# Order of the recurrence's square roots, of the first up-projection operands and of the right operands in a hybrid decoder layer

## The chip, the cores and the metric

The kernel runs on one core of a Trainium2 chip. The metric is the device time of one execution in microseconds (us). Before the change, three runs gave 1567.91, 1569.7 and 1569.8 us, median 1569.7.

A core has five engines that run side by side, each with its own queue, taken in order: TensorE (PE: matmuls, and PEld, its weight loads), VectorE (DVE), ScalarE (ACT), GpSimd (POOL, used here only to issue DMAs that add while they copy) and SyncE (SP, which issues the other DMAs). An instruction waits at the head of its queue until the semaphores it names have been raised; what stands behind it waits too.

## The reference

One layer on x of 1024 positions by 1024 channels, all in float32:

```
h = rms_norm(x, g_mix);  z = h @ w_in + b_in        # 7168 columns: va, ga, xb, gb, sa, sb
u = silu(layer_norm(conv31(va * sigmoid(ga))));  y_a = u @ w_a_out
v = conv4(xb)                                        # 1536 channels
r, i = sigmoid(v @ w_rg_a + b), sigmoid(v @ w_rg_x + b)   # block diagonal, 16 heads of 96
log_a = -8 r softplus(-lam);  a = exp(log_a);  mult = sqrt(-expm1(2 log_a)), 1 at the first position
h_t = a_t h_(t-1) + mult_t i_t v_t                   # the recurrence
y_b = (h * gelu(gb)) @ w_b_out
x1 = x + (sigmoid(sa) * y_a + sigmoid(sb) * y_b) @ w_o
x2 = x1 + relu(rms_norm(x1, g_mlp) @ w_1)^2 @ w_2
out = rms_norm(x2, g_final)
```

## The kernel before

Every float32 operand of a matmul is kept as a high and a low part in the matmul's own format, and a product is three matmuls (high x high, high x low, low x high). The high part is a conversion on ACT; the low part is a subtraction on DVE, or, in `split_dma` (L63 to L67), a negated copy on ACT (L65) to which a DMA issued by POOL adds the source (L66), followed by the high part on ACT (L67). Larger products are done by a Strassen-like scheme: seven block products, numbered p = 1 to 7, whose left and right operands are sums of blocks.

The order on each engine is written out by hand (`manual_schedule`): the instructions stand in the queues in the order in which the program names them. Only the place of the convolution's taps among other work on DVE is set by a plan: `clk` holds estimated times of PE, ACT and DVE, `later` (L640) puts work with a due time on a list, and `vector_work` (L644) and `fill` (L385) put as many taps ahead of each piece of work as its due time leaves room for. A tap is one multiply-add over some 500 elements (L581). A convolution is begun by two scaled copies on ACT (L563, L564).

**Stage one** (L746 to L803) goes through slots s = 3 to 27. In a slot PE does one chunk of z, 128 channels by 1024 positions, as 48 matmuls of 128x512 (`chunk_mm`, L661): 32 with the high part of the chunk's weights, `win_h`, then 16 with the low part, `win_l`. Slots with a head add twice six matmuls of 96x512 for its two gates (`head_mm`, L472); the gates' PSUM tile `rg` exists once, so the second gate's matmuls wait until ACT has read the first (`head_gate`, L482 to L486). In the slot ACT also takes the chunk before out of PSUM (`xb_out`, L415 to L422: bias, then the first tap of the width-4 convolution; its three other taps are on DVE, L430), makes the weights of the next slot (`w_parts`, L656), and the parts of v (`xb_parts`, L436), which wait for the taps on DVE.

The heads come in four groups of four, and after each group stand two slots for the recurrence of its three tiles of 128 channels: in the first (EXP in L740) `scan_exp` (L497) does three times an Exp and a Tanh at the end of ACT's work in that slot; in the second `scan_root` (L506) does three square roots (L510), last in ACT's work of that slot. Exp and Tanh, Sqrt, and the sigmoid each need their own function table, which ACT loads when the kind changes. `scan_tile` (L517) on DVE then does the scan of a tile; its due time in the plan comes from `rooted`, which `scan_root` sets. In the fourth group the slot after Exp and Tanh has no xb chunk to take out and no head behind it.

**The MLP's first steps.** `gseq` (L1110) runs the products of w_a_out, of w_o and the first two block products of w_1 ("u", p = 1 and 2, for the first four pairs of column blocks); GX (L1483 to L1512) lists by step what else is put into the queues. At the steps u0 and after, x1 of the odd positions is transposed to rows (`x1_rows`, L1284: PE, squares on ACT, copies on DVE), its root is found (`x1_root`, L1310; `x1_diag`, L1318), a PE step spreads it over all partitions (`x1_spread`, L1331, tile `rbm`), and eight products on DVE normalize x1 (`x1_normed`, L1341). Then come the sums of the right operand (`g_t`, L1132; n = 1 to 4), their parts (`g_parts`, L1121: operands gu6, gu5, gu7, gu3 by ACT and DVE, gu4 by `split_dma`) and the left operands of the first two pairs (`up_load`, L1373, loads a block of w_1; `up_lhs`, L1383, makes the sums s1, s2, s4 on DVE and the parts by `split_dma`). The tiles for these sums are five in all. `useq` (L1580) then runs the other block products: for the first two pairs p = 6, 5, 7, 3, 4 in turn (PSUM tiles f0b, f1b, f0c, f1c, f0d, f1d, and f0c, f1c, f0d, f1d again), then the pairs 2, 3 and so on (f2b is the first); UX (L1583) lists what goes beside its first steps. PE begins f0b right behind the last "u" product.

Of the kernel before, what the change touches and what calls it, by code (L numbers as in the profile page):

```python
# [30 lines left out]
def trunk_kernel(ctx: ExitStack, tc: tile.TileContext, x, xt_in, xt_eo, vecs, w_in, w_a_out, w_b_out,  # L31
# [15 lines left out]
    def PS(name, tag="ps"):  # L47
        return pp.tile([P, S], F32, tag=tag, name=name, bufs=1 if tag == "ps2" else 3)
# [330 lines left out]
    def at(e, cost, ready=0.0):  # L379
        clk[e] = max(clk[e], ready) + cost  # L380
        return clk[e] + 0.1
# [33 lines left out]
    def xb_out(t, ps):  # L415

        a = T(f"xb{t}")
        nc.scalar.activation(a, ps, AF.Identity, bias=bin_c[:, XB + t:XB + t + 1])
        v = T(f"v{t}")
        w = WB - 1  # L420
        nc.scalar.activation(v, a, AF.Identity, scale=cbw_c[:, w * 12 + t:w * 12 + t + 1],  # L421
                             bias=cbb_c[:, t:t + 1])  # L422
        ready = at("A", 2.35)
        vt[t] = v

        def rest():
            for d in range(1, WB):

                w = WB - 1 - d
                nc.vector.scalar_tensor_tensor(v[:, d:S], a[:, 0:S - d],  # L430
                                               cbw_c[:, w * 12 + t:w * 12 + t + 1], v[:, d:S],
                                               ALU.mult, ALU.add)

        later(ready, 3.8, rest)
# [37 lines left out]
    def head_mm(n, gi):  # L472
        vh, vl = parts[n]
        gh, gl = gws[n]
        gps[n, gi] = ps = PS(f"rg{n}_{gi}", "ps2")
        for hf, hs in enumerate(HALVES):
            o = ps[:HD, hs]
            nc.tensor.matmul(o, gh[:, gi, :], vh[:, hs], start=True, stop=False)
            nc.tensor.matmul(o, gl[:, gi, :], vh[:, hs], start=False, stop=False)
            nc.tensor.matmul(o, gh[:, gi, :], vl[:, hs], start=False, stop=True)  # L480
        at("P", 6 * MM)

    def head_gate(n, gi, ready):
        g, hh = divmod(n, 4)
        a = H(f"g{n}_{gi}", "g")
        nc.scalar.activation(a, gps.pop((n, gi))[:HD, :], AF.Sigmoid,  # L486
                             bias=(ba_c, bx_c)[gi][:, n:n + 1])
        at("A", 1.11, ready)
        for (ti, p0, p1, d0) in PIECES[hh]:
            t = 3 * g + ti  # L490
            if (gi, t) not in gate:
                gate[gi, t] = T(f"g{gi}_{t}")
            nc.sync.dma_start(gate[gi, t][p0:p1, :], a[d0:d0 + p1 - p0, :])
# [12 lines left out]
    def scan_root(g):  # L506
        at("A", 2.56)
        for t in range(3 * g, 3 * g + 3):
            r = gate[0, t]
            nc.scalar.activation(r, r, AF.Sqrt)  # L510
            rooted[t] = at("A", 1.06)
# [17 lines left out]
    def u_out(j, psv, psg):  # L529

        u = T(f"u{j}")
        uv = u.rearrange("p (o n) -> p o n", o=2)
        nc.scalar.activation(uv, psg.rearrange("p (n o) -> p o n", o=2), AF.Sigmoid,
                             bias=bin_c[:, GA + j:GA + j + 1])
        later(at("A", 1.11), 1.28, nc.vector.scalar_tensor_tensor, uv,
              psv.rearrange("p (n o) -> p o n", o=2), bin_c[:, VA + j:VA + j + 1], uv,
              ALU.add, ALU.mult)
        ut[j] = u
        fresh.append(j)
# [104 lines left out]
    def vector_work(end):  # L644
        for ready, _, cost, f, a in sorted(todo, key=lambda x: x[:2]):
            dve(cost, ready, f, *a)
        todo.clear()
        taps["wait"] += fresh
        fresh.clear()
        fill(end)  # L650

    def w_load(s):
        if s < NC1:
            wraw[s] = load_w(w_in[CH[s]], f"win{s}")

    def w_parts(s):  # L656
        if s < NC1:
            wst[s] = split_w(wraw.pop(s), [P, 8, P], f"win{s}")
            at("A", 2.1)

    def chunk_mm(s, n0, n1):  # L661

        wh, wl = wst[s]
        if n0 == 0:
            zps[s] = PS(f"z{s}")
        pairs = [x for k in range(8) for x in ((wh, k, 0), (wh, k, 1))] + [(wl, k, 0) for k in range(8)]
        for n in range(n0, n1):
            w, k, part = pairs[n]
            for hf in range(2):
                nc.tensor.matmul(zps[s][:, HALVES[hf]], w[:, k, :], xw[k][part][hf],  # L670
                                 start=n == 0, stop=n == 23)
        at("P", 2 * (n1 - n0) * MM)
# [67 lines left out]
    EXP = {head_slot: g for g, head_slot in enumerate(HS0[4 * g + 3] + 1 for g in range(4))}  # L740
# [5 lines left out]
    with tc.manual_schedule(engines=ENGINES):  # L746
        for s in range(3, NC1):
            w_load(s + 2)
            taps["hold"] = s > NC1 - 4
            begun = clk["P"]  # L750
            clk["A"], clk["V"] = max(clk["A"], begun + 0.5), max(clk["V"], begun - 2)

            chunk_mm(s, 0, 18)
            before, new, nxt = (head_at.get(s + d) for d in (-1, 0, 1))
            if before is not None:

                head_gate(before, 0, begun)
                head_mm(before, 1)
            chunk_mm(s, 18, 24)
            if new is not None:  # L760
                head_mm(new, 0)

            c = CH[s - 1]
            if s == 3:
                xb_out(0, zps[0])
            if c >= XB:
                xb_out(c - XB, zps[s - 1])
            elif c >= GA:
                u_out(c - GA, zps[s - 2], zps[s - 1])
            w_parts(s + 1)  # L770
            if s == 3 or c >= XB:
                vector_work(0)
                xb_parts(0 if s == 3 else c - XB)
            if before is not None:
                head_gate(before, 1, clk["P"] - 12 * MM)
            if nxt is not None:
                head_w_parts(nxt)
            if s + 2 in head_at:
                head_w(head_at[s + 2])
            for d in range(5):  # L780
                if s - d in EXP:
                    g = EXP[s - d]
                    if d == 0:
                        scan_exp(g)
                        scan_in(begun + 3.5, 3 * g, 3 * g + 1)
                    elif d == 1:
                        scan_in(begun + 3.5, 3 * g + 2)
                        scan_root(g)

                    t = 3 * g + d - (2 if g < 3 else 1)  # L790
                    if 3 * g <= t < 3 * g + 3 and t < 11:
                        later(rooted[t], 4.8, scan_tile, t)
            if s == NC1 - 1:
                z_get(0, z_lhs)
                z_get(1, z_lhs)
            for f, *a in XS.get(s, ()):
                f(*a)
            if s == NC1 - 3:
                for i in range(4):
                    z_load(i // 2, i % 2)  # L800
            vector_work(clk["P"] - 0.7)
            if nxt is not None:
                head_load(nxt)  # L803
# [676 lines left out]
    def g_get(n, f):  # L1480
# [18 lines left out]
        10: ((g_t, "o", 0, 4), (x_in2, 1, 2, 3)), 11: ((g_t, "o", 1, 4),), 12: ((g_parts, "o", 4, 0),),  # L1499
        13: ((g_parts, "o", 4, 1),), 15: ((g_parts, "o", 5, 0),), 16: ((g_parts, "o", 5, 1), (up_load, 0, (0,))),  # L1500
        17: ((g_parts, "o", 3, 0), (up_load, 1, (0,))), 18: ((g_parts, "o", 3, 1), (up_load, 2, (0,))),
        19: ((up_load, 3, (0,)),), 20: ((x1_rows, 0, 1),), 21: ((x1_rows, 2, 3),), 22: ((x1_diag, 0),),
        23: ((x1_spread, 0), (x1_normed, 0, 0)), 24: ((g_parts, "u", 1, 0), (g_parts, "u", 1, 1)),
        25: ((x1_normed, 1, 0),), 26: ((g_parts, "u", 2, 0),), 27: ((g_parts, "u", 2, 1),)}.items()})
    u0 = 2 * o0
    GX.update({u0 + n: v for n, v in {
        0: ((x1_rows, 4, 5, 6, 7),), 1: ((up_load, 0, (1,)),),
        2: ((x1_diag, 1), (x1_spread, 1), (up_load, 1, (1,))),
        3: ((x1_normed, 0, 1), (x1_normed, 1, 1), (g_t, "u", 0, 1), (g_t, "u", 1, 1)),
        4: ((g_t, "u", 0, 2), (g_t, "u", 1, 2)), 5: ((g_parts, "u", 6, 0), (up_lhs, 0, 6)),  # L1510
        6: ((g_parts, "u", 6, 1), (up_lhs, 1, 6), (g_parts, "u", 5, 0), (up_lhs, 0, 5)),
        7: ((g_parts, "u", 5, 1), (up_lhs, 1, 5), (g_t, "u", 0, 3), (g_t, "u", 1, 3))}.items()})  # L1512
    with tc.manual_schedule(engines=ENGINES):
        for j in range(8):
            clk["A"], clk["V"] = max(clk["A"], clk["P"] + 0.5), max(clk["V"], clk["P"] - 2)
# [48 lines left out]
        for n in range(len(gseq) + 1):  # L1564
# [15 lines left out]
    useq = [(i, p) for p in ORDER[1:4] + (3, 4) for i in range(2)]  # L1580
    useq += [(i, p) for i in range(2, AHEAD) for p in ORDER[1:4] + (3, 4)]
    useq += [(i, p) for i in range(AHEAD, NP) for p in ORDER]
    UX = {0: ((g_parts, "u", 7, 0), (g_t, "u", 0, 4)), 1: ((g_parts, "u", 7, 1), (g_t, "u", 1, 4)),  # L1583
          2: ((g_parts, "u", 4, 0),), 3: ((g_parts, "u", 3, 0), (g_parts, "u", 4, 1)),
          4: ((g_parts, "u", 3, 1),)}
    KC = 2
    NC_ = NP // KC
    BLK = {11: 0, 22: 1, 21: 2, 12: 3}
# [88 lines left out]
    with tc.manual_schedule(engines={mybir.EngineType.Activation, mybir.EngineType.DVE,  # L1677
                                     mybir.EngineType.PE}):
        for n in range(len(useq)):
# [4 lines left out]
            while ready < min(len(useq), n + look + 1):  # L1684
# [4 lines left out]
                ready += 1  # L1689
            for f, *a in UX.get(n, ()):  # L1690
                f(*a)
# [111 lines left out]
    g = g_  # L1803
# [141 lines left out]
```

## Time and profile before

| | |
|---|---|
| median of three runs | 1569.7 us (1567.91 to 1569.8) |
| the profiled execution | 1569.0 us, span of its instructions 1567.0 us |
| granted TensorE clock, mean | 0.997 |
| PE busy | 1543.2 us, 98% of the span |
| ACT, DVE, POOL busy | 893.5, 1211.7, 187.5 us |
| DMA | 309.38 MB, mean 197 GB/s |
| longest waits of PE | 7.1 us at the start (for the first squares on ACT), then 2.0 us in three pieces at `rg` |

A line of a timeline gives the start in us from the span's start, the length in us, the engine, the line of the kernel, the operation, output<-inputs by the program's names without buffer numbers, partitions x elements, how many; in brackets the idle time of that engine just before, and what ended it. Matmuls follow each other before the one before has left the array, so a matmul that is listed with 0.39 us takes 0.227 us of PE's time in a row of its like. A line of the waits gives who waited for what, and then us in total, times, and the longest.

### The profile page before, as it was taken

To read this page: it belongs to the slowest core of one execution; us is meant where nothing else is said; L and a number is where in the kernel's file an instruction comes from. 1 tells how busy PE (TensorE), PEld (TensorE's weight loads), DVE (VectorE), ACT (ScalarE), POOL (GpSimd) and SP (SyncE) were. 2 spreads that over 40 slices of the span, in tenths; PEclk is the share of its full clock that TensorE was granted. 3 is DMA by queue.
4 is the path that set the end of the run, shared out by engine and by line. 5 is a ranking of instruction groups with operands and counts; after the bars stand their busy time and mean duration, and the time that the engine had idled before them with its cause. 6 is when DMAs were issued, how large, how long until landed. Compare 5 with 4: busy or idle time off the path is not lost. (4 is left out here: it accounts for less than half of the span.)

```text
span 1567.0 us, 19218 instructions
## 1 busy us (share of the span) xinstructions
PE 1543.2 (98%) x6830; PEld 1267.1 (81%) x6830; DVE 1211.7 (77%) x1631; ACT 893.5 (57%) x1251; POOL 187.5 (12%) x222
## 2 busy tenths in 40 slices
PE   8999999999999999999999999999999999999997
PEld 6888778788888888888888887788888888888886
DVE  6799999979999997468579868765555558888897
ACT  5547575667667666445275777544444475555552
POOL 0000000002222222000022323000000001111110
PEclk9999999999999999999999999999999999999999
DMA  9667878899998878953579878533333779888852
GB/s 371 166 156 185 227 177 219 206 279 233 240 248 214 192 188 233 315 177 108 179 203 304 195 170 201 172 108 108 108 108 114 239 224 228 219 225 227 203 122 107
DMA packets 128799, 309.38 MB, mean 197 GB/s; under 512 B 12944, under 2 KB 30864, under 8 KB 128704
## 3 DMA queue, kind: packets, MB, share of 16 engines
q1 hardware_dynamic: 97824, 230.59, 44.9%
q0 software_dynamic: 30736, 77.31, 27.1%
q8 instruction: 53, 0.87, 0.2%
q14 instruction: 42, 0.34, 0.1%
q10 hardware_dynamic: 144, 0.26, 0.1%
HBM read 147.69 MB, written 58.72 MB: 132 GB/s over the span
## 5 line engine op out<-in xcount | busy, mean ns | idle before, releaser
L670 PE MATMUL z<-xh,win_h 128*128 128x512 f32 x400 | 123.4, 390 | 0.0
L670 PE MATMUL z<-xl,win_h 128*128 128x512 f32 x400 | 123.2, 389 | 0.0
L1738 DVE TENSOR_TENSOR acc<-acc,d 128x1024 f32<-128x1024 f32 x72 | 87.8, 1220 | 33.3 <-PE d L1726 32.7
L670 PE MATMUL z<-xh,win_l 128*128 128x512 f32 x400 | 98.1, 391 | 0.0
L670 PEld LDWEIGHTS z<-xh,win_l 128*128 128x128 f32 x400 | 75.0, 188 | 17.2 <-DMA win_l<-win_raw 0.4
L581 DVE SCALAR_TENSOR_TENSOR y<-u,vec,y 128x511 f32<-128x511 f32 (+14 forms) x120 | 88.5, 737 | 0.0
L670 PEld LDWEIGHTS z<-xh,win_h 128*128 128x128 f32 x400 | 75.1, 188 | 16.2
L670 PEld LDWEIGHTS z<-xl,win_h 128*128 128x128 f32 x400 | 75.1, 188 | 15.8
L486 ACT ACTIVATE g<-rg,vec 96x1024 f32<-96x1024 f32 x32 | 35.6, 1111 | 84.5 <-PE rg L480 46.6
L581 DVE SCALAR_TENSOR_TENSOR yt<-u,vec,yt 128x511 f32<-128x511 f32 (+6 forms) x112 | 82.7, 738 | 0.0
L581 DVE SCALAR_TENSOR_TENSOR y<-yt,csum,y 128x511 f32<-128x511 f32 (+6 forms) x112 | 82.7, 738 | 0.0
L66 POOL DMA_DIRECT2D win_l<-win_raw x25 | 21.8, 872 | 315.4 <-ACT win_l L65 239.0
L1410 ACT ACTIVATE o<-s 128x512 fp32r<-128x512 f32 x56 | 33.8, 624 | 44.8 <-DVE s L1395 29.7
L430 DVE SCALAR_TENSOR_TENSOR v<-xb,vec,v 128x1023 f32<-128x1023 f32 (+2 forms) x36 | 46.2, 1282 | 16.5 <-ACT v L421 15.7
L1024 PE MATMUL yb<-hgh,wb_h 128*128 128x512 f32 x168 | 52.6, 394 | 0.0
L66 POOL DMA_DIRECT2D zo<-zw x42 | 36.8, 878 | 127.3 <-ACT zo L65 114.8
L1024 PE MATMUL yb<-hgl,wb_h 128*128 128x512 f32 x168 | 51.8, 389 | 0.0
L66 POOL DMA_DIRECT2D db_1l<-wr x7 | 6.1, 876 | 309.8 <-ACT db_1l L65 253.9
L1024 PE MATMUL yb<-hgh,wb_l 128*128 128x512 f32 x168 | 41.0, 389 | 0.0
L65 ACT ACTIVATE zo<-zw 128x512 fp32r<-128x512 f32 x42 | 26.3, 625 | 20.7 <-PE z5f L841 2.1
L1024 PEld LDWEIGHTS yb<-hgh,wb_h 128*128 128x128 f32 x168 | 31.5, 188 | 7.4 <-issue 1.0
L990 DVE TENSOR_TENSOR o<-s,o 128x512 fp32r<-128x512 f32 x56 | 37.3, 683 | 0.0
(1778 smaller groups left out, 4666.2 us busy)
## 6 DMA issues: line engine op xcount, KB each, us to landing
w_raw<-in_w_dram SPq DMA_DIRECT2D x34, 512.0 KB, 5.6
fr<-fd SPq DMA_DIRECT2D x32, 512.0 KB, 5.8
wr<-in_w_dram SPq DMA_DIRECT2D x32, 512.0 KB, 6.6
zw<-in_w_in_dram SPq DMA_DIRECT2D x28, 512.0 KB, 5.8
win_raw<-in_w_in_dram SPq DMA_DIRECT2D x25, 512.0 KB, 7.1
win_l<-win_raw POOLq DMA_DIRECT2D x25, 512.0 KB, 6.1
zo<-zw POOLq DMA_DIRECT2D x42, 256.0 KB, 5.7
gates<-zg SPq DMA_DIRECT2D x32, 256.0 KB, 3.9
```

Source lines behind the costliest of these rows:

```text
L65: nc.scalar.activation(l, src, AF.Copy, scale=-1.0)
L66: nc.gpsimd.dma_start(l, src, accum_op=ALU.add)
L430: nc.vector.scalar_tensor_tensor(v[:, d:S], a[:, 0:S - d], cbw_c[:, w * 12 + t:w * 12 + t + 1], v[:, d:S], ALU.mult, ALU.add)
L486: nc.scalar.activation(a, gps.pop((n, gi))[:HD, :], AF.Sigmoid, bias=(ba_c, bx_c)[gi][:, n:n + 1])
L581: nc.vector.scalar_tensor_tensor(o[:, k:], a[:, 0:HS - k], c, o[:, k:], ALU.mult, add)
L670: nc.tensor.matmul(zps[s][:, HALVES[hf]], w[:, k, :], xw[k][part][hf], start=n == 0, stop=n == 23)
L990: tt(l, src, h.bitcast(F32), ALU.subtract)
L1024: nc.tensor.matmul(ps[hf], a, b[:, HALVES[hf]], start=n == 0, stop=n == len(todo) - 1)
L1410: nc.scalar.activation(o[:, 0], src, AF.Copy)
L1738: tt(acc[p, q2], acc[p, q2], ps, ALU.add)
```

## The change

Three moves; no instruction is added or taken away. First, `scan_root` is called ahead of the slot's other ACT work instead of behind it: it stands between the slot's first matmuls and `xb_out`, so that the roots follow the last Tanh directly on ACT. Its estimate `rooted` is earlier with it, and so more taps stand ahead of some work on DVE; in the fourth group the two copies that begin a convolution then stand ahead of the roots on ACT. Second, w_1's odd blocks of the first two pairs are loaded eight steps earlier, and the left operands p = 6 and 5 of these pairs are made one to five steps after u0 instead of five to seven, the first two of them (p = 6) beside the root of x1. Third, in UX the seventh operand's two parts are made at once, then the third's, and the fourth sum (`g_t` 4) and the fourth operand behind them.

```
@@ stage one @@
                 head_mm(before, 1)
+            if s - 1 in EXP:
+                scan_root(EXP[s - 1])
             chunk_mm(s, 18, 24)
...
                     elif d == 1:
                         scan_in(begun + 3.5, 3 * g + 2)
-                        scan_root(g)
@@ GX, from o0 = 28 @@
-        19: ((up_load, 3, (0,)),), 20: ((x1_rows, 0, 1),), 21: ((x1_rows, 2, 3),), 22: ((x1_diag, 0),),
+        19: ((up_load, 3, (0,)),), 20: ((x1_rows, 0, 1),), 21: ((x1_rows, 2, 3), (up_load, 0, (1,))), 22: ((x1_diag, 0), (up_load, 1, (1,))),
@@ GX, from u0 = 56 @@
-        0: ((x1_rows, 4, 5, 6, 7),), 1: ((up_load, 0, (1,)),),
-        2: ((x1_diag, 1), (x1_spread, 1), (up_load, 1, (1,))),
+        0: ((x1_rows, 4, 5, 6, 7),), 1: ((up_lhs, 0, 6),),
+        2: ((x1_diag, 1), (x1_spread, 1), (up_lhs, 1, 6)),
         3: ((x1_normed, 0, 1), (x1_normed, 1, 1), (g_t, "u", 0, 1), (g_t, "u", 1, 1)),
-        4: ((g_t, "u", 0, 2), (g_t, "u", 1, 2)), 5: ((g_parts, "u", 6, 0), (up_lhs, 0, 6)),
-        6: ((g_parts, "u", 6, 1), (up_lhs, 1, 6), (g_parts, "u", 5, 0), (up_lhs, 0, 5)),
-        7: ((g_parts, "u", 5, 1), (up_lhs, 1, 5), (g_t, "u", 0, 3), (g_t, "u", 1, 3))}.items()})
+        4: ((g_t, "u", 0, 2), (g_t, "u", 1, 2), (up_lhs, 0, 5)), 5: ((g_parts, "u", 6, 0), (up_lhs, 1, 5)),
+        6: ((g_parts, "u", 6, 1), (g_parts, "u", 5, 0)),
+        7: ((g_parts, "u", 5, 1), (g_t, "u", 0, 3), (g_t, "u", 1, 3))}.items()})
@@ UX @@
-    UX = {0: ((g_parts, "u", 7, 0), (g_t, "u", 0, 4)), 1: ((g_parts, "u", 7, 1), (g_t, "u", 1, 4)),
-          2: ((g_parts, "u", 4, 0),), 3: ((g_parts, "u", 3, 0), (g_parts, "u", 4, 1)),
-          4: ((g_parts, "u", 3, 1),)}
+    UX = {0: ((g_parts, "u", 7, 0), (g_parts, "u", 7, 1)), 1: ((g_parts, "u", 3, 0), (g_t, "u", 0, 4)),
+          2: ((g_parts, "u", 3, 1), (g_t, "u", 1, 4)), 3: ((g_parts, "u", 4, 0),),
+          4: ((g_parts, "u", 4, 1),)}
```

## The prediction

> **What bounds the kernel now.** I read the page first, then the list of waits of TensorE, then the timelines of the stretches that the edits touch.
>
> ```profile
> PE 1543.2 (98%) x6830; PEld 1267.1 (81%) x6830; DVE 1211.7 (77%) x1631; ACT 893.5 (57%) x1251; POOL 187.5 (12%) x222
> ```
>
> TensorE (PE) is the bound: 1543.2 of 1567.0 us. An edit of order on other engines matters only where it removes or makes a wait of PE. The waits that the change can reach:
>
> ```profile
> PE rg L478 <- ACT g L486: 2.0, 3, 0.7
> PE f0b L1422 <- DMA o<-s: 1.5, 1, 1.5
> ...
> PE f0b L1422 <- DVE gu6l L990: 0.5, 1, 0.5
> ```
>
> (Columns: us in total, times, longest.) The first is the gate matmul of a head that follows a recurrence slot, three times; the others are the first steps of the up projection. What the second stretch costs in all is seen on PE's own timeline, with one step as the chain of waits has it:
>
> ```profile
> 956.44 0.39 PE L1422 MATMUL f0b<-gu6h,o 128*128 128x512 f32 x1
> ...
> 986.91 0.50 PE L1422 MATMUL f0d<-gu4l,o 128*128 128x512 f32 x1 [0.31 <-DMA gu4l<-x]
> ...
> 991.76 0.39 PE L1422 MATMUL f2b<-gu6h,o 128*128 128x512 f32 x1
> 994.65 2.72 PE f2c L1422 x12
> ```
>
> Ten steps stand between 956.44 and 991.76: 35.3 us, where ten times 2.72 is 27.2. So 8.1 us at most are to be had there, and 3 x 0.84 = 2.5 at the heads (worked out below).
>
> **Part one, the square roots.** ScalarE (ACT) in the first of four groups, and PE beside it:
>
> ```profile
> 144.42 1.15 ACT L503 ACTIVATE g<-g,sm 128x1024 f32<-128x1024 f32 x1
> 145.48 1.10 ACT L418 ACTIVATE xb<-z,vec 128x1024 f32<-128x1024 f32 x1
> ...
> 148.71 1.04 ACT L67 ACTIVATE win_h<-win_raw 128x1024 fp32r<-128x1024 f32 x1
> 151.90 1.06 ACT L438 ACTIVATE vth<-v 128x1024 fp32r<-128x1024 f32 x1 [2.15 <-DVE v L430]
> ...
> 153.23 1.28 ACT L510 ACT_TABLE_LOAD   x1
> 154.52 2.96 ACT L510 ACTIVATE g<-g 128x1024 f32<-128x1024 f32 x3
> 157.50 1.28 ACT L486 ACT_TABLE_LOAD   x1
> 158.79 1.11 ACT L486 ACTIVATE g<-rg,vec 96x1024 f32<-96x1024 f32 x1
> ```
>
> ```profile
> 150.93 0.63 PE L670 MATMUL z<-xh,win_h 128*128 128x512 f32 x2
> ...
> 158.21 1.07 PE L670 MATMUL z<-xh,win_l 128*128 128x512 f32 x4
> 159.96 0.48 PE L478 MATMUL rg<-vh,rgh 96*96 96x512 f32 x1 [0.68 <-ACT g L486]
> ```
>
> Today the table load and three roots stand last in the slot, from 153.23 to 157.50: 4.27 us. The change puts them right behind the last tanh (144.42). ACT has no idle time there: xb follows at once. So xb, v and the two parts of the next slot's weights, win_l and win_h, all come 4.27 later. win_h then ends at 148.71 + 4.27 + 1.04 = 154.02, and PE's next slot, which begins with win_h, wanted it at 150.93. PE stands until about 154.1 (at 159.96 it began 0.06 after the gate's end): **3.15 us** of new wait, where there were 1.18 of slack.
>
> What is gained? The 2.15 idle before vth is a wait for VectorE's taps on v, and v itself comes 4.27 later, so the idle time moves along and nothing is hidden in it: vth at 156.17 and rgh, then the table load, and the gate at about 158.8 as before. PE's wait for it does go, since PE comes late: it would have passed at 158.21 + 4 x 0.227 (2.72 / 12) = 159.12, lost 0.84, and now arrives at 154.1 + 8.2 = 162.3, after the gate's end at 159.90. Net +2.3 a group. VectorE gets eight more taps ahead of v; they fill the longer wait and delay v by about 0.1, which by then nobody feels. The third group shows the same spacing:
>
> ```profile
> 282.14 1.04 ACT L67 ACTIVATE win_h<-win_raw 128x1024 fp32r<-128x1024 f32 x1
> ```
>
> ```profile
> 284.37 0.63 PE L670 MATMUL z<-xh,win_h 128*128 128x512 f32 x2
> ```
>
> Slack 1.19 again, so three groups give 3 x 2.3 = **+6.9**. The fourth group has no xb and no gate behind it, but the new order also puts the two starts of a convolution in front of the roots:
>
> ```profile
> 265.14 0.80 ACT L563 ACTIVATE y<-u,vec 128x512 f32<-128x512 f32 x1
> 265.85 0.71 ACT L564 ACTIVATE yt<-u,vec 128x512 f32<-128x512 f32 x1
> ...
> 346.36 1.04 ACT L67 ACTIVATE win_h<-win_raw 128x1024 fp32r<-128x1024 f32 x1
> ```
>
> ```profile
> 349.67 0.62 PE L670 MATMUL z<-xh,win_h 128*128 128x512 f32 x2
> ```
>
> win_h ends at 346.36 + 1.4 + 4.27 + 1.04 = 353.1, PE wanted it at 349.67: **+3.4**, and no wait goes in return. The moved step also issues the DMA that completes win_l:
>
> ```profile
> DMA to landing us min/median/max: 4.5/6.1/10.3
> ```
>
> win_l is written by 153.1 in group one and needed at 154.1 + 7.3 = 161.4; with the median it lands near 159.5, with the longest near 163.7. So it costs nothing up to 2 us each; I take 0, and 0.5 in the fourth group, where the queues are full. POOL's queue has nothing else in it there; on SP's queue the loads of a later head wait for v's low part some 4 us longer, and that head runs a slot later.
>
> **The clock.** A wait of PE has a second price in this trace (columns: window, us, busy of PE, PEld, DVE, ACT, POOL, granted clock, DMA share, GB/s):
>
> ```profile
> 960.00:961.00 1.00, 0.49 (x1) 0.50 (x2) 1.00 (x2) 1.00 (x3) 0.66 (x1) 0.58 1.03 180
> 961.00:962.00 1.00, 1.00 (x4) 0.71 (x4) 1.00 (x2) 0.97 (x3) 0.21 (x1) 0.50 0.76 129
> ...
> 963.00:964.00 1.00, 1.00 (x5) 0.80 (x4) 1.00 (x2) 1.00 (x3) 0.53 (x1) 0.72 0.83 281
> ...
> 978.00:980.00 2.00, 0.86 (x4) 0.24 (x2) 0.40 (x1) 1.57 (x3) 0.87 (x1) 1.00 1.11 271
> 980.00:982.00 2.00, 1.24 (x6) 0.95 (x6) 2.00 (x3) 0.00 (x0) 0.00 (x0) 1.00 1.06 206
> ```
>
> After the waits of 1.5 and 0.5 the granted clock was halved from about 960.2 to 963.6; that costs 1.7 us. At 978 to 982 about 1.9 us of idle time in two pieces left it at 1.00. So the bounds for a wait of 3 us are 0 and 1.7. It lies beyond both rows; I take 1.3, nearer the first, since a wait can straddle what the clock is judged by. Four waits: **+5.2** (0 to 6.8).
>
> [...]
>
> **Part two, the first up operands.** They are made earlier, between the row copies and the normalization, whose root PE needs:
>
> ```profile
> 939.01 0.15 DVE L1313 TENSOR_TENSOR stm<-stm 128x4 f32<-128x4 f32 x1
> ...
> 952.80 0.69 DVE L1394 TENSOR_TENSOR s<-w_raw 128x512 f32<-128x512 f32 x1
> ```
>
> ```profile
> 940.07 0.27 ACT L1315 ACTIVATE stm<-stm 128x4 f32<-128x4 f32 x1
> ...
> 954.24 0.63 ACT L65 ACTIVATE o<-s 128x512 fp32r<-128x512 f32 x1 [1.40 <-DVE s L1395]
> 954.78 0.62 ACT L67 ACTIVATE o<-s 128x512 fp32r<-128x512 f32 x1
> ```
>
> ```profile
> 941.84 1.11 PE L1336 MATMUL rbm<-rdm,ones 128*128 128x128 f32 x8
> ```
>
> ```profile
> o<-s POOLq DMA_DIRECT2D x8, 256.0 KB, 3.3
> gu<-w_raw POOLq DMA_DIRECT2D x5, 256.0 KB, 7.7
> ```
>
> The change does not put the sums into the wait for the root; three of them (0.7 each) come ahead of L1313, at 939.01, and the two conversions of their result (0.5 each) ahead of the root on ACT. The second sum ends near 940.4, the conversions near 941.5, u1 follows, and the root runs near 942.05 instead of 940.07. PE has no slack at rbm (it runs on from the matmul before), so it waits about **2.0 us** there. Then VectorE makes two sums of the second pair, and its third, which reuses a buffer that the first pair's DMA still reads, waits for that DMA, issued near 941.4: it lands at 944.7 to 949.1 by the two rows. The eight normalizing products stand behind it and start at 946 to 950 instead of near 943. Six sums and the DMA waits leave the way to f0b in return: I get f0b's first operand at 956 to 959.6, and PE there at 958.4. On SP's queue the loads of w_1 that the sums read move up among the row stores and may hold these until a buffer of the o stage is free; the stores are read only much later. On POOL's queue the new DMA goes ahead of two that PE needs only a step of four matmul groups later. So f0b's 1.5 and most of its clock loss go, and the two waits for the third right operand (now converted ahead of the fourth) go too. What is late next is the fourth operand's low part: its conversion moves little (the conversions taken out ahead of f0b are 3 us, ACT starts 3 to 4 later), and today it was issued at
>
> ```profile
> 976.93 0.87 POOL L66 DMA_DIRECT2D gu4l<-x  x1 [1.54 <-ACT gu4l L65]
> ```
>
> and PE waited for it at 986.91. PE, 3 us ahead by then, waits for it longer, and f2b begins near 991 to 992 as today. **0 us** is what I take; the bounds: -4.6 if this DMA needs 6.1 us instead of 10, +4.5 if the products start at 950 and the clock is halved twice.
>
> **Sum.** 6.9 + 3.4 + 0.5 + 5.2 + 0 = +16.0 on the profiled execution's 1569.0 us (span 1567.0), which lies 0.7 below the median: **1585 us**. Between and behind the two stretches PE is busy throughout, so nothing gives it back.
>
> **Rivals.** (a) The clock holds in all four waits: for it speak the rows at 978, against it that each wait here is one piece of 3 us or more. 6.9 + 3.9 = +10.8, less up to 4 us if the up stretch gains: 1576 to 1580. [...] (b) The up stretch gets worse: products at 950, a halved clock after rbm and again after gu4l: +4.5, and win_l late: 1590 to 1595. (c) Faster: ACT finds room for the roots. Place: between tanh and win_h; it decides where win_h comes less than 1.2 us later, for then PE never waits for weights, the heads' 2.5 go and the up stretch may give 4.6: 1562. Against it: ACT runs without a gap from tanh to win_h, and a load and three roots measure 4.27. (d) The edits cancel, or the order on the queues does not do what I read: within 0.2% of before, about 1569.
>
> **How the numbers follow.** My forecast, 1580 to 1590, has 0.52; (a) 0.23; (b) 0.15; (c) 0.07; (d) 0.03. The range 1574 to 1592 holds the forecast, (a) and about a third of (b): 0.8. Faster by over 0.2% (3.1 us, about what a measurement of this kernel can tell from no change): 0.07; within it: 0.03; slower: 0.90.
>
> **What would show it.** Right: four waits of PE at L670 for ACT win_h, three near 3.0 and one near 3.4 us, none left at rg L478, granted clock of 0.5 behind most of them; a wait of 2 us at rbm; f0b's wait gone and a longer one at f0d for gu4l. Wrong: no wait at L670 (then part one's step fails), clock at 1.00 behind them (a), f2b less than 30 us behind f0b's place (part two gains). PE's steps from f2b on should be unchanged.

## The result, and the profile after

| | before | after |
|---|---|---|
| median of four runs each | 1569.47 us (1567.91 to 1569.8) | 1591.94 us (1590.5 to 1593.12) |
| the profiled execution, its span | 1569.0, 1567.0 us | 1590.5, 1588.7 us |
| granted TensorE clock, mean | 0.997 | 0.993 |

The ratio is 1.0145 (95% interval 1.0127 to 1.0162): the change costs 22.5 us in the median and 21.7 in the two profiled spans; 16.0 were forecast. The profiled execution of the kernel after is the fastest of its four (granted clock 0.993, the others 0.990 to 0.992), so the shares below are those of this execution.

The first line of the page, and then TensorE's waits in the kernel after:

```profile
PE 1549.7 (98%) x6830; PEld 1272.0 (80%) x6830; DVE 1211.2 (76%) x1631; ACT 894.8 (56%) x1251; POOL 187.4 (12%) x222
```

```profile
PE z L670 <- ACT win_h L67: 12.1, 4, 3.2
PE f0d L1423 <- DMA gu4l<-x: 7.2, 2, 4.0
...
PE rbm L1337 <- DVE rdm L1327: 1.8, 1, 1.8
PE f0b L1423 <- DVE gu6l L991: 1.0, 2, 0.8
```

The four waits for `win_h`, the one at `rbm` and the longer ones for `gu4l` are there; the three at `rg` are not. PE also counts 6.5 us more of busy time with the same 6830 matmuls: some ran at half clock. Where the span grows is read from places that both timelines have: the start of a "u" product behind stage one, the step at which PE reaches the fourth right operand, and the step f2b, from which the prediction said that nothing changes. Before:

```profile
936.27 0.47 PE L1187 MATMUL gu1a<-gu1h,gu 128*128 128x512 f32 x1
...
984.85 0.39 PE L1422 MATMUL f0d<-gu4h,o 128*128 128x512 f32 x1
```

and after:

```profile
951.71 0.47 PE L1188 MATMUL gu1a<-gu1h,gu 128*128 128x512 f32 x1
...
959.25 1.13 PE L1337 MATMUL rbm<-rdm,ones 128*128 128x128 f32 x8 [1.80 <-DVE rdm L1327]
...
997.47 0.39 PE L1423 MATMUL f0d<-gu4h,o 128*128 128x512 f32 x1
1001.84 0.69 PE L1423 MATMUL f0d<-gu4l,o 128*128 128x512 f32 x1 [3.98 <-DMA gu4l<-x]
...
1007.84 0.51 PE L1423 MATMUL f0d<-gu4l,o 128*128 128x512 f32 x1 [3.18 <-DMA gu4l<-x]
...
1013.47 0.39 PE L1423 MATMUL f2b<-gu6h,o 128*128 128x512 f32 x1
```

Up to the "u" products the kernel after is 951.71 - 936.27 = 15.4 us late; at f0d it is only 12.6 late (997.47 against 984.85), because f0b's wait for the DMA, the halved clock behind it and the waits for gu3 are gone, while 1.8 us at `rbm` and half a microsecond more for gu6l at f0b were added; at f2b it is 21.7 late (1013.47 against 991.76), and stays so to the end. So stage one costs 15.4, the up stretch 6.3 in all, and within that the two steps with the fourth operand alone 9.1. Of the 15.4, 0.4 stand there ahead of anything that was edited: the last gate matmul ahead of the first late slot begins at 150.70 before and at 151.12 after, and at 150.35 to 151.87 in the traces below. So a difference of about 1 us in such a place between two kernels need not be an effect of their edits.

ACT in the first group, after, is what the prediction laid out: load and roots ahead of xb, `win_h` until 154.43, and the idle time before `vth` moved along instead of filled:

```profile
146.01 1.28 ACT L510 ACT_TABLE_LOAD   x1
147.31 2.96 ACT L510 ACTIVATE g<-g 128x1024 f32<-128x1024 f32 x3
...
153.39 1.04 ACT L67 ACTIVATE win_h<-win_raw 128x1024 fp32r<-128x1024 f32 x1
156.60 1.06 ACT L438 ACTIVATE vth<-v 128x1024 fp32r<-128x1024 f32 x1 [2.17 <-DVE v L430]
```

The clock behind the waits, in windows of the kernel after (the granted clock is the third figure from the right; a window of 1 us with 0.74 was halved for the last 0.52 us of it):

```profile
155.00:156.00 1.00, 1.00 (x5) 0.77 (x5) 0.96 (x2) 0.00 (x0) 0.00 (x0) 0.74 1.00 193
156.00:157.00 1.00, 1.00 (x4) 0.81 (x3) 1.00 (x2) 0.40 (x1) 0.00 (x0) 0.50 1.06 201
158.00:159.00 1.00, 1.00 (x4) 0.74 (x3) 1.00 (x2) 1.00 (x1) 0.00 (x0) 0.55 0.00 0
225.00:226.00 1.00, 0.86 (x4) 0.71 (x5) 0.96 (x2) 0.09 (x1) 0.47 (x1) 1.00 0.00 0
226.00:227.00 1.00, 1.00 (x6) 0.82 (x5) 1.00 (x1) 0.00 (x0) 0.00 (x0) 1.00 1.02 197
295.00:296.00 1.00, 1.00 (x5) 0.74 (x4) 0.96 (x2) 0.00 (x0) 0.00 (x0) 0.71 1.06 201
363.00:364.00 1.00, 0.25 (x1) 0.25 (x2) 1.00 (x3) 0.70 (x1) 0.87 (x1) 0.85 0.97 342
```

Behind the first, third and fourth wait the clock is halved, for 3.41 us each time; behind the second, which is as long as the first (2.95 and 2.96 us), it is not.

### The profile page after: what moved, and what is told of

It is laid out like the page before. It is cut to its first block, busy times and chain, and to the rows that moved or that the text cites. A ratio compares the mean times of both kernels' runs of the same rounds, so it can differ in the third digit from the quotient of the medians.

```text
span 1588.7 us, 19216 instructions
## 1 busy us (share of the span) xinstructions
PE 1549.7 (98%) x6830; PEld 1272.0 (80%) x6830; DVE 1211.2 (76%) x1631; ACT 894.8 (56%) x1251; POOL 187.4 (12%) x222
## 5 line engine op out<-in xcount | busy, mean ns | idle before, releaser
L670 PE MATMUL z<-xh,win_h 128*128 128x512 f32 x400 | 126.6, 398 | 12.1 <-ACT win_h L67 12.1
L670 PEld LDWEIGHTS z<-xh,win_h 128*128 128x128 f32 x400 | 76.5, 192 | 30.3 <-ACT win_h L67 13.9
```

## Experiments

Two theories stood at the beginning. Mine: the two parts are separate; stage one loses by the late `win_h` and the clock, the up stretch by the way of `gu4l`, that is by UX and not by the early operands. The rival: what is late in stage one, or the early operands, makes the up stretch late.

**The roots alone.** The kernel before with the first hunk of the diff only.

> The kernel before with the square roots moved and nothing else. Theory: the loss of stage one is the late win_h alone (four waits of PE of about 3 us, three waits at rg gone, and a halved clock behind three of the four), 15.4 us by the place where PE begins the up products in the trace after; so 1585 us (1583 to 1587), and PE's steps behind stage one unchanged. Rival one: the loss in the up stretch is a consequence of the roots' place as well; then the roots alone make all of it, 1592 us. Rival two: the halved clock in the trace after is chance of that execution; then 1580 us.

1588.31 us against 1569.56 (ratio 1.0113, 1.0098 to 1.0128): above the theory's range, below the rival's 1592. In the trace the waits for `win_h` are the same to the tenth, but gu1a begins 17.5 us late, not 15.4, and f2b 17.6: the up stretch loses 0.1 (in it a new wait of 1.2 us for gu7l at f0d stands against the halved clock behind f0b, 0.50 from 960.15 to 963.56 before, which is missing here). The clock was halved for five stretches of 3.41 us in stage one, not for three. So the parts are separate, and the price of the clock isn't fixed.

**The up part, whole and in halves.** The kernel before with the hunks of GX and UX together, and with each alone.

> The kernel before with the moved up operands (GX) and the third right operand ahead of the fourth sum (UX), the roots where they were. Theory: +6.3 us, made of 2.0 at rbm, minus 2.2 at f0b, minus 2.5 at gu3, and plus 9 at the two waits for gu4l with their halved clock; 1576 us (1573 to 1579). Rival: the up stretch loses only because stage one shifts it against the DMA queues; then 1569 to 1570 us, as the prediction took it.

> The kernel before with the up operands made earlier (GX) and UX as before. Theory: the early operands cost 2.0 at rbm and give 2.2 at f0b, and gu4 is still converted ahead of gu3, so the waits for gu4l stay under 1 us: 1568 to 1571 us. Rival: the early operands are what is wrong (the sum that waits for the DMA of the first pair holds the eight products and everything behind them): then this kernel has most of the 6 us, 1574 to 1577 us.

> The kernel before with the third right operand ahead of the fourth sum and the fourth operand last (UX), the early up operands left out. Theory: gu4's DMAs are issued about 3 us later and each behind the DMA of a left operand; the waits of gu3 (1.9 us) go, and two waits for gu4l of 3 to 6 us with a halved clock come: 1575 to 1579 us. Rival: the late gu4l needs the early operands' DMAs too, in the same queue; then 1567 to 1570 us.

Together 1577.19 us (1.0044, 1.0029 to 1.0059), GX alone 1568.42 (0.9991, 0.9982 to 1.0001), UX alone 1578.09 (1.0048, 1.0033 to 1.0063), against 1569.56. In the traces f2b moves by +7.3, -1.2 and +9.3 us, of the last 1.1 from before the "u" products (1.2 of delay is there at the gate matmul at 150.70 already, so it is none of UX). All three times lie in the theory's ranges: the early operands cost nothing on balance (1.8 lost at `rbm`, more than that won at f0b), and the loss comes with UX. Not all of it is gu4l's in UX alone: its two waits for gu4l are 2.2 and 4.0 us, and a wait of 2.0 us at f0c for the sum `fa` on DVE stands in this kernel only. In UX alone, the DMAs of the fourth operand on POOL are issued at

```profile
975.68 0.87 POOL L66 DMA_DIRECT2D o<-w_raw  x1 [1.12 <-ACT o L65]
977.15 0.87 POOL L66 DMA_DIRECT2D gu4l<-x  x1 [0.60 <-ACT gu4l L65]
978.61 0.87 POOL L66 DMA_DIRECT2D o<-w_raw  x1 [0.59 <-ACT o L65]
980.08 0.87 POOL L66 DMA_DIRECT2D gu4l<-x  x1 [0.60 <-ACT gu4l L65]
```

In the kernel before, the second gu4l was issued at 976.93 and the first at 973.04; now a left operand (o<-w_raw) stands ahead of each in the queue. On ACT both conversions of gu3 and one of o4 have gone ahead of gu4l.

**The order in POOL's queue.** In steps 3 and 4 of `useq`, UX is taken ahead of the left operands:

```
+            for f, *a in UX.get(n, ()) if n in (3, 4) else ():
+                f(*a)
             while ready < min(len(useq), n + look + 1):
...
-            for f, *a in UX.get(n, ()):
+            for f, *a in UX.get(n, ()) if n not in (3, 4) else ():
                 f(*a)
```

> The changed kernel, with the two parts of the fourth operand put ahead of the left operands p = 4 in the same steps, so that the DMA of each gu4l goes into POOL's queue ahead of that of o4 (as before the change: gu4, o4, gu4, o4). Theory: the place in the queue is a part of the loss; gu4l is issued 1.5 us earlier with 256 KB less ahead of it, so the two waits of 4.0 and 3.2 us shrink to about half and one halved clock goes: 1587 to 1589 us. Rival: the engines of the DMA are full either way and the four transfers end together as late as now; f1d then waits for o4 what f0d no longer waits for gu4l: 1591 to 1592 us.

1590.03 us (1.0140, 1.0125 to 1.0155): nothing that the runs can tell from the kernel after. The trace has the rival's picture, for the most part: PE waits less for gu4l and instead for the transfer that went behind it.

```profile
PE f0d L1423 <- DMA gu4l<-x: 2.7, 2, 1.5
PE f0d L1423 <- DMA o<-w_raw: 2.1, 1, 2.1
```

The up stretch costs 5.3 instead of 6.3 us. The second gu4l was issued by 992.67 and reached at 1005.40, 12.7 us later, although the order is that of the kernel before. Order alone is a small part.

**gu4's low part without a DMA.** `if w == "u" and p in (2, 4)` in `g_parts` becomes `p == 2`, so VectorE makes it.

> The changed kernel, with the low part of the fourth operand made by VectorE, as for the third, instead of by a negated copy and an adding DMA. Theory: the up stretch loses through the way of gu4l over the DMA alone; without it both waits of f0d go, with their halved clock, and f2b comes about 9 us earlier: 1582 to 1584 us. Rival: VectorE is late as well (its sums stand in the same queue as the results that it takes from PSUM); then f0d waits for gu4l 2 to 4 us all the same: 1586 to 1590 us.

1582.96 us (1.0091, 1.0076 to 1.0106), as the theory has it. No wait for gu4l is left, and from gu1a to f2b the kernel is 3.8 us faster than before. Its profiled execution was its slowest run, 1585.95 us, and shows why stage one is hard to price; the windows behind the first wait (which ended at 154.31):

```profile
153.00:155.00 2.00, 0.69 (x2) 0.60 (x3) 1.96 (x2) 1.25 (x2) 0.87 (x1) 0.67 0.00 0
155.00:157.00 2.00, 2.00 (x6) 1.57 (x5) 1.96 (x3) 0.58 (x1) 0.00 (x0) 0.50 1.06 203
157.00:159.00 2.00, 2.00 (x6) 1.60 (x5) 1.95 (x4) 1.98 (x3) 0.00 (x0) 0.50 0.32 59
159.00:161.00 2.00, 2.00 (x7) 1.54 (x7) 1.90 (x4) 1.99 (x3) 0.00 (x0) 0.62 0.70 256
```

The clock is halved from 153.7 to 160.5, twice 3.41 us, and seven such stretches stand behind the four waits; gu1a began 20.7 us late with the same four waits for `win_h` as in the kernel after (and one of 0.6 us at the start of the kernel, which the others do not have).

**The roots in ACT's idle time.** `scan_root` is called behind `w_parts(s + 1)` instead of ahead of `chunk_mm(s, 18, 24)`.

> The changed kernel, with the roots called behind the next slot's weights and ahead of v's parts, that is in the 2.15 us in which ScalarE waits for v. Theory: what the roots cost in stage one, they cost as the work that stands ahead of win_h; so the four waits and their halved clocks go (15 to 18 us), and as 2.15 of the 4.27 us of load and roots are hidden, the gate comes 2 us earlier and the three waits at rg (2.5 us) stay away: 1571 to 1574 us. Rival: v's parts, 2.1 us later, hold the loads of the head's operands, and the head waits instead: 1576 us or more.

1573.44 us (1.0026, 1.0016 to 1.0037), the theory's range. ACT in the first group:

```profile
148.35 1.05 ACT L67 ACTIVATE win_h<-win_raw 128x1024 fp32r<-128x1024 f32 x1
149.42 1.28 ACT L510 ACT_TABLE_LOAD   x1
150.71 2.96 ACT L510 ACTIVATE g<-g 128x1024 f32<-128x1024 f32 x3
153.57 1.05 ACT L438 ACTIVATE vth<-v 128x1024 fp32r<-128x1024 f32 x1
```

`win_h` comes as early as before, the 2.15 us of waiting for v are filled, and neither wait exists: gu1a begins at 932.95, 3.3 us ahead of before. Moving the same roots past the weights turns 15.4 us of loss into a gain. The up stretch costs 6.4 us here (f2b begins at 994.85), as in the kernel after, so its loss does not come from stage one's delay.

**Work in the wait.** Twelve matmuls on operands that are there go ahead of the slots with the late `win_h`; they write the slot's accumulator, which its first product overwrites.

```
             zps[s] = PS(f"z{s}")
+            if s - 2 in EXP:
+                for n in range(12):
+                    nc.tensor.matmul(zps[s][:, HALVES[n % 2]], xw[0][0][0][:, 0:P], xw[0][0][0],
+                                     start=True, stop=True)
```

> The changed kernel, with twelve matmuls more (2.7 us) put in front of the four slots whose win_h comes late, into the accumulator that the slot then overwrites: TensorE works through the wait, and win_h comes no earlier. Theory: what is behind the waits is the granted clock, halved for 3.4 us behind three of them (1.7 us each); busy through the wait it stays at 1.00, and the time falls by 5 us: 1586 to 1588 us. Rival: the clock drops for another reason than the idle time, or the matmuls delay the slot: 1591 us or more.

1588.91 us (1.0131, 1.0114 to 1.0148): 0.9 us above the theory's range and below the rival's. The clock did stay at 1.00 behind the first wait (154 to 159 us), behind the fourth two matmuls take 0.46 us from 360.87 on, as at full clock, and the execution's granted clock is 0.996 against 0.993 in the kernel after; but a new wait took a part of the gain:

```profile
PE z L674 <- DMA win_l<-win_raw: 1.6, 1, 1.6
...
PE z L674 <- ACT win_h L67: 1.2, 4, 0.5
```

That is the fourth group's win_l, which PE reached 7.6 us after it began the slot and got 9.2 after (360.29 and 369.50). In the kernel after, with 3.4 us of the slot at half clock, PE reached it 9.0 us after the slot's begin (363.75 and 372.71) and did not wait; that the slower clock hid the wait is inferred from these figures. Here gu1a is 12.4 us late (it begins at 948.68); less the 1.6 this is 10.8. The prediction's terms without clock and win_l add to 10.3 (6.9 + 3.4).

**Half the work in the wait.** Six matmuls instead of twelve.

> The changed kernel with six matmuls more (1.4 us) ahead of the four slots whose win_h comes late, so that of each wait about half is left: three waits of 1.6 us and one of 1.8. [...] So here it stays at 1.00 behind the first three waits wherever the grid lies, and is halved behind the fourth at most: 2 to 3 us below the changed kernel, 1588 to 1590 us, as with twelve matmuls. Rival: any wait of this place halves the clock, the shorter idle time only moves it; then it shows 0.50 behind at least two of the first three, 1591 us or more.

1588.17 us (1.0117, 1.0100 to 1.0134): the theory's range. Two of the four waits, and the windows behind the first and the last of them:

```profile
154.93 0.73 PE L674 MATMUL z<-xh,win_h 128*128 128x512 f32 x2 [1.59 <-ACT win_h L67]
...
360.95 0.93 PE L674 MATMUL z<-xh,win_h 128*128 128x512 f32 x2 [1.84 <-ACT win_h L67]
```

```profile
154.00:156.00 2.00, 1.07 (x5) 0.89 (x6) 1.93 (x3) 0.88 (x1) 0.87 (x1) 1.00 0.19 37
156.00:158.00 2.00, 2.00 (x10) 1.66 (x9) 2.00 (x2) 0.96 (x1) 0.00 (x0) 1.00 1.09 209
360.00:362.00 2.00, 1.05 (x3) 0.92 (x4) 1.90 (x4) 0.90 (x1) 0.87 (x1) 0.83 0.98 298
362.00:364.00 2.00, 2.00 (x6) 1.54 (x6) 1.97 (x2) 1.06 (x1) 0.00 (x0) 0.50 0.98 331
```

1.00 behind the waits of 1.6 us, halved behind that of 1.84: the three waits of 1.6 us cost their idle time and no halved clock. The grid in the forecast was an estimate from four traces: the runs show the distances between the drops of the clock (last section), not what decides which wait is followed by one.

**Why gu4l is late.** Still open was why a DMA that was forecast at 10 us takes more. In the kernel after, on POOL:

```profile
988.65 0.87 POOL L66 DMA_DIRECT2D o<-w_raw  x1 [1.12 <-ACT o L65]
990.12 0.87 POOL L66 DMA_DIRECT2D gu4l<-x  x1 [0.60 <-ACT gu4l L65]
991.59 0.87 POOL L66 DMA_DIRECT2D o<-w_raw  x1 [0.59 <-ACT o L65]
993.06 0.87 POOL L66 DMA_DIRECT2D gu4l<-x  x1 [0.60 <-ACT gu4l L65]
```

From the end of the issue to the matmul that waits for it: 1001.84 - 990.99 = 10.9 us for the first, 1007.84 - 993.93 = 13.9 for the second; before it was 986.91 - 977.80 = 9.1 for the second. (The first was read there without a wait at 985.08, at most 11.2 us after its issue by 973.91, so only the second is shown to take longer now.) One kernel takes both o4 out of the queue (their low parts by VectorE: `if i < 2` in `up_lhs` becomes `if i < 2 and p != 4`), one issues gu4 earlier and ahead of them:

```
-    UX = {0: ((g_parts, "u", 7, 0), (g_parts, "u", 7, 1)), 1: ((g_parts, "u", 3, 0), (g_t, "u", 0, 4)),
-          2: ((g_parts, "u", 3, 1), (g_t, "u", 1, 4)), 3: ((g_parts, "u", 4, 0),),
-          4: ((g_parts, "u", 4, 1),)}
+    UX = {0: ((g_parts, "u", 7, 0), (g_parts, "u", 7, 1)), 1: ((g_parts, "u", 3, 0), (g_t, "u", 0, 4)),
+          2: ((g_parts, "u", 4, 0), (g_t, "u", 1, 4)), 3: ((g_parts, "u", 4, 1), (g_parts, "u", 3, 1))}
```

> The changed kernel with the low parts of the left operands p = 4 of the first two pairs by VectorE, so that the two gu4l stand in POOL's queue without the two o4 (512 KB less) and nothing else of gu4 is changed. Theory: gu4l takes 11 and 14 us because o4 stands ahead of it; without it it takes 7 to 9 us, the two waits of f0d shrink from 7.2 to 1 to 3 us with one halved clock or none: 1585 to 1587 us. Rival: it takes so long because the loads of w_1 fill the DMA engines at the time; then gu4l still takes 11 us or more, and 1589 to 1592 us are measured.

> The changed kernel with the fourth operand's parts one step earlier, ahead of both o4 and of the third operand's second half: its DMAs are issued some 2.5 to 3 us earlier and first in the queue. Theory: the loss is the late issue together with the place in the queue; the two waits shrink from 7.2 to about 2 us, the third operand's second half costs 0.5 to 1 us of wait at f0c: 1586 to 1588 us. Rival: the adding DMA has a time of its own of 10 to 14 us that begins with the issue, so the waits shrink by no more than the 3 us of the issue and the clock is still halved twice: 1589 us or more.

1589.52 us (1.0130, 1.0113 to 1.0147) and 1590.88 (1.0134, 1.0119 to 1.0150): both times lie in the rivals' ranges, but can't speak for them, since stage one's clock moves by more than what is asked (gu1a begins 19.4 us late in the first kernel's trace; the second kernel's four runs go from 1586.83 at a granted clock of 0.994 to 1591.95 at 0.989). The traces answer, and they are nearer to the theories than to the rivals. From gu1a to f2b the two lose 1.7 and 1.8 us against 6.3 in the kernel after. Without o4 in the queue:

```profile
1003.60 0.50 PE L1423 MATMUL f0d<-gu4l,o 128*128 128x512 f32 x1 [1.75 <-DMA gu4l<-x]
1007.39 0.79 PE L1423 MATMUL f0d<-gu4l,o 128*128 128x512 f32 x1 [2.13 <-DMA gu4l<-x]
```

gu4l was issued by 994.46 and 996.88 there and took 9.1 and 10.5 us, where 7 to 9 were expected, and the waits are 3.9 us, not 1 to 3: o4 in the queue made up 1.7 and 3.4 of 10.9 and 13.9. Issued earlier and ahead of o4:

```profile
PE f0d L1423 <- DMA gu4l<-x: 2.0, 2, 1.2
...
PE f0d L1423 <- DMA o<-w_raw: 1.0, 1, 1.0
PE f0c L1423 <- DVE gu3l L991: 0.5, 1, 0.5
```

Here the issue came 1.6 us earlier, not 2.5 to 3, and the transfers took 10.1 and 11.3 us (issued by 989.37 and 992.31, reached at 999.50 and 1003.57). That is within the rival's 10 to 14, but the waits for gu4l shrank by 5.2 us, more than the issue moved, and one stretch of clock was halved, not two. So the late issue and what stands ahead in the queue each account for a part. What is left without o4 in the queue, 9.1 and 10.5 us for 512 KB each, and why the second transfer takes 11.3 to 12.7 with the order of the kernel before and took 9.1 there, was not taken apart.

**A version that beats both.** Three kernels: the kernel after with the roots in ACT's idle time and gu4's low part by VectorE; then the same with the first pair's sums behind the diagonal of x1's root and the second pair's behind the eight products; and the kernel before with nothing but the roots in the idle time. The edit that makes the second out of the first:

```
-        0: ((x1_rows, 4, 5, 6, 7),), 1: ((up_lhs, 0, 6),),
-        2: ((x1_diag, 1), (x1_spread, 1), (up_lhs, 1, 6)),
-        3: ((x1_normed, 0, 1), (x1_normed, 1, 1), (g_t, "u", 0, 1), (g_t, "u", 1, 1)),
+        0: ((x1_rows, 4, 5, 6, 7),),
+        2: ((x1_diag, 1), (x1_spread, 1), (up_lhs, 0, 6)),
+        3: ((x1_normed, 0, 1), (x1_normed, 1, 1), (up_lhs, 1, 6), (g_t, "u", 0, 1), (g_t, "u", 1, 1)),
```

> The changed kernel with the roots behind the next slot's weights and with gu4's low part by VectorE. Theory: the two causes are separate and add up: stage one 3.3 us shorter than before (the waits at rg gone, none for win_h), the up stretch 3.8 shorter (no wait at gu3 nor gu4l, 1.8 still lost at rbm): 1562 us (1560 to 1564). Rival: what is saved in stage one is lost again at the up stretch, because there TensorE comes earlier against DMAs that run at the same time: 1565 us or more.

> As the kernel with both edits (roots behind the next slot's weights, gu4's low part by VectorE), and the sums of the first pair put behind the diagonal of x1's root instead of ahead of the root, those of the second pair behind the eight products. Theory: the 1.8 us at rbm are there because three sums and two conversions stand ahead of the root; they go, and gu6 comes about 1 us late at f0b: 1 us below the kernel with both edits. Rival: VectorE is the bound between the root and f0b, and the wait only moves from rbm to f0b: the same time within 0.7 us.

> The kernel before with the roots behind the next slot's weights, in the time in which ScalarE waits for v, and nothing else. Theory: the gate comes 2 us earlier, three waits of PE at rg (0.84 each with what PE loses beside them) go, and nothing new comes: 2.5 to 3.3 us below before, 1566 us. Rival: the up stretch swallows it: within 1 us of before.

1563.26 us (0.9958, 0.9945 to 0.9970), 1561.00 (0.9947, 0.9935 to 0.9960) and 1566.52 (0.9977, 0.9968 to 0.9986) against 1570.00. The first lies in the theory's range, the last 0.2 us below it. Stage one gained less in the first than forecast (gu1a 1.9 us ahead of before, 2.6 without the 0.7 by which the gate matmul was late already, not 3.3), and in the last a new wait of 0.6 us for win_l came. The second's wait at `rbm` is gone, and f0b's grew by half a microsecond:

```profile
PE f0b L1423 <- DVE gu6l L991: 1.6, 2, 0.8
PE f0d L1423 <- DMA o<-w_raw: 0.5, 1, 0.5
```

From gu1a to f2b it is 4.9 us faster than before, the first 3.6: the edit is worth 1.3 in the traces, nearer to the theory's 1 than to the rival, but the intervals of the two overlap.

## Why the prediction was right in its direction and too low

- **The late win_h, right.** Three waits of 3.0 and one of 3.4 were forecast, 2.95 to 2.96 and 3.19 measured; the heads' waits at `rg` went. With the clock held up, stage one lost 10.8 us besides win_l, against 10.3 forecast.
- **win_l, too small, and hidden.** 0.5 was forecast for the fourth group; 1.6 measured where PE comes on time, none in the kernel after.
- **The clock, right in the sum by luck.** 1.3 a wait, 5.2 in all, was taken; 15.4 less 10.8 leaves 4.6 in the profiled execution, where one of the four waits had no halved clock behind it. But the bounds, 0 to 1.7 a wait, were wrong: in other executions with the same four waits it was 6.7 and 9.9 (17.5 and 20.7 less 10.8), up to 2.5 a wait, because a wait can be followed by two halved stretches (6.83 us at 0.50 from 294.25 on with the roots alone). Each stretch costs 1.3 to 1.5 us (4.6 for three, 6.7 for five, 9.9 for seven).
- **rbm, f0b and gu3, right.** 2.0 forecast at `rbm`, 1.80 of wait and 2.0 of delay measured; the third sum of the second pair did wait for the first pair's DMA (1.7 us, until 962.23, or 946.8 less the 15.4; 944.7 to 949.1 forecast); f0b's DMA wait and the two for gu3 are gone, and PE was 2.8 us ahead at f0d (3 forecast).
- **The step that failed: "PE, 3 us ahead by then, waits for it longer, and f2b begins near 991 to 992 as today. 0 us is what I take".** f2b began 6.3 us behind stage one's delay. The two steps with the fourth operand took 16.0 us (997.47 to 1013.47) where they took 6.9 before: 6.3 more of waits and 2.8 of halved clock. I held gu4l's landing fixed. But its issue moved (against stage one's delay by 1.6 and 0.7 us, since gu3 and o4 are now converted ahead of it), and the second transfer took 13.9 us instead of 9.1. Without this DMA the loss is gone. Without o4 in the queue the second transfer takes 10.5, with the issue 1.6 us earlier and the old order 11.3, with the old order alone 12.7. So both the issue and the queue have a part, and why even then it takes longer than before the change stays open. The bounds -4.6 to +4.5 did not hold +6.3: the upper one put its loss into late products, with one halved clock behind `rbm` and one behind gu4l, not into two late transfers. (How -4.6 came about isn't shown; 10 less 6.1 is 3.9.)
- **The rivals.** (a) is out for these waits. (b) has the time in its range but not by its mechanism: the eight products began at 947.4 (962.84 less 15.4), not 950, no clock was halved behind `rbm`, and win_l was not late. (c) is out for the place that the change gave the roots: ACT has no room ahead of `win_h`. Its condition, that `win_h` comes in time, holds with the roots behind `win_h`, and there stage one gains 1.9 to 3.3 us in four traces.

## What to carry to other kernels

Moving work ahead in an in-order queue delays everything that it passes; look for the engine's own idle time behind the last operand that the bound engine needs, and put the work there: the same 4.27 us cost 15.4 us ahead of the four instructions that end with `win_h` and gained 1.9 to 3.3 behind them. When a wait goes, ask what the queue behind the next operand looks like in the new order (issue time, what stands ahead in the DMA queue), instead of carrying its old landing time over. And a wait of TensorE has a second price here, the halved clock, that differed between executions with the same waits (4.6, 6.7 and 9.9 us); kernels with such waits need several executions before a difference of 5 us is believed.

## What the runs showed of the hardware

In the profiled execution after, read in windows of 0.1 us, the granted clock drops to 0.50 at 155.48, 295.43 and 363.69 us, and behind gu4l at 1001.99 and 1008.81; every drop lasts 3.41 us, and the distances are 41, 20, 187 and 2 times 3.413 us. In the traces of the roots alone (drops at 154.31, 225.99, 294.25, 365.93), of gu4 by VectorE (153.69, 225.37, 297.05, 368.73) and of o4 by VectorE (154.00, 225.68, 293.95, 365.63) all distances are 20 or 21 times 3.413, and the drops last 3.41 or 6.83 us; at f0d one of 10.24 us begins at 1001.28 with the turned order in POOL's queue and one at 999.61 with six matmuls in the wait.

Six traces have the late `win_h` with nothing put into the wait (the kernel after, the roots alone, the turned order in POOL's queue, gu4 by VectorE, o4 by VectorE, gu4 issued earlier). Of their 24 waits 20 were followed by a halved clock, seven of them for 6.83 us. All but one of the 24 were of 2.95 to 3.2 us, the other of 4.0. The second wait of the kernel after is one of the four that were not:

```profile
225.14 0.74 PE L670 MATMUL z<-xh,win_h 128*128 128x512 f32 x2 [2.95 <-ACT win_h L67]
```

It runs from 222.19 to 225.14, and 20 times 3.413 us behind the drop at 155.48 is 223.75, inside the wait: 1.56 us of idle time ahead of it, 1.39 behind it, and the clock stayed at 1.00. The first wait of the same trace, which was followed by a drop, runs from 151.52 to 154.48, and 155.48 less 3.413 is 152.07: 0.55 us ahead of it, 2.41 behind it. That this division decides is my estimate from such pairs; no run changed it alone. Of shorter idle time the runs show single cases: with six matmuls in the wait three of 1.58 to 1.59 us kept 1.00 and one of 1.84 did not. In the kernel before, the two pieces of 1.49 and 0.52 us at f0b were followed by a drop at 960.15, the two of 1.14 and 0.76 us at 978 to 981, shown in the prediction's rows, were not.
